# Slot transposes and slot weights from one bfloat16 product a quad, with the late one-hots formed in bfloat16 on VectorE

## The chip, the core and the metric

The kernel runs on one core of a Trainium2 chip. The metric is device time in microseconds; three runs of the kernel before took 504.05 us in the median (504.04 to 505.17). The engines are TensorE (PE; its weight loads are PEld), VectorE (DVE), ScalarE (ACT), GpSimd (POOL) and SyncE (SP, which only issues DMAs here).

## What is computed

A two-layer trunk for 256 tokens of width 1024. Each layer is a mixer and a mixture of experts (MoE), each followed by a layer norm of sqrt(2) times the input plus the result. The change lies in the MoE, which stands once in each layer:

```python
gate = jnp.sum(jax.nn.one_hot(expert_id, MOE_EXPERTS, dtype=f32) * weights[..., None], axis=1)
y = jnp.zeros((n_tok, d), f32)
for e in range(MOE_EXPERTS):
    hid = jax.nn.silu(t @ w_gate[e]) * (t @ w_up[e])
    y = y + gate[:, e:e + 1] * (hid @ w_down[e])
```

There are 16 experts in 4 groups. A router picks one group and two of its experts for each token, so all but two of a token's 16 gates are zero.

## The kernel before

The kernel doesn't compute every expert on every token. It cuts the tokens into two tiles of 128 (t = 0, 1) and gives every expert 32 slots in each tile, 512 slots in all. Four experts form a quad (q = 0 to 3), so a quad has 128 slots a tile.

For each tile, `rank` (L977) finds the slot numbers `pos` of a token's two experts, and `places` (L999) forms the one-hot matrix P of 128 tokens by 512 slots: `places(t, 0)` the columns of quads 0 and 1, `places(t, 1)`, later, those of quads 2 and 3. Products with P gather the tokens of the slots, transposed, into XT (`gather`, L1045). For each quad, `gate_up` (L1088) multiplies XT by the gate and up weights into the PSUM bank gu; `act` (L1100) forms sg = silu(gate) on ScalarE and hd = sg times up on VectorE; `turn` (L1108) transposes hd on TensorE (bank ht), and ScalarE copies it to hT; `down_mm` (L1119) multiplies by the down weights (bank dn); `weigh_hi` and `weigh_lo` multiply by the slot weight ws and split the result into a rounded part and a rest; `combine` adds PT times that to the tokens' sums. PT is P transposed by quads, and ws is the slot's gate, brought from token order into slot order.

`slots` (L1064) makes PT and ws. For each tile, TensorE transposes P in four pieces by the identity in fp32 (bank pt), and ScalarE copies the bank to PT; TensorE then multiplies each piece of P by rghl, the 16 gates of each token in two rounded parts (bank wsp), and VectorE adds the two parts and picks, for each of the four groups of 32 slots, the column of its own expert.

The order is written out by hand; each engine carries its instructions out in that order, and semaphores let one wait for another. Around the first quad it is: gates of both tiles, act of tile 0, the late halves of P, gate/up products of tile 1, its act, then on TensorE turn(0), slots(0), slots(1), turn(1) and the down products:

```python
        gates(0)
        gates(1)
        most()
        sc.preload_act_table_set(SILU)
        act(0, 0)
        places(0, 1)
        places(1, 1)
        acc = [None, None]
        gate_up(0, 1, range(8))
        act(0, 1)
        turn(0, 0)
        slots(0)
        slots(1)
        turn(0, 1)
        both(down, 0, 0)
```

PSUM banks for gu, ht, pt, wsp and dn come from one pool of four, so a bank's next writer waits for the last reader of what it held. Weights come in through a ring of 19 SBUF buffers that SP fills in order; two of the first quad's weight tiles (wh) are loaded by GpSimd's queue. After the gates, a token count (rcnti) is loaded into a register by every engine, for a branch on overfull experts that isn't taken with these inputs.

Of the kernel before, what the change touches and what calls it, by code (L numbers as in the profile page):

```python
# [9 lines left out]
F32 = mybir.dt.float32  # L10
F32R = mybir.dt.float32r
BF16 = mybir.dt.bfloat16
I32 = mybir.dt.int32
U32 = mybir.dt.uint32
AF = mybir.ActivationFunctionType
OP = mybir.AluOpType
# [25 lines left out]
for _n, _w in [("ident", 128), ("triU", 128), ("ntriSL", 128), ("sbT", 128),  # L42
               ("fold", 32), ("sel", 16), ("cosk", 32), ("sink", 32), ("ropeT", 256),
               ("e32p", 16), ("grp", 16), ("iota", 256), ("mssd", 128), ("msb", 128), ("mfox", 128), ("mmla", 128),
               ("ltri", 128), ("e32", 16)]:
    CC[_n] = (_o, _o + _w)
    _o += _w
NCC, NC0 = _o, CC["mssd"][0]
# [10 lines left out]
def constants():  # L59
    c = np.zeros((128, NCC), np.float32)  # L60

    def put(n, a):
        c[:a.shape[0], CC[n][0]:CC[n][1]] = a

    i = np.arange(128)
    r, k = i[:, None], i[None, :]
    f = np.float32
    put("ident", (r == k).astype(f))
    put("triU", (r <= k).astype(f))
    put("ntriSL", -(r > k).astype(f))  # L70
    put("sbT", -(r >= k).astype(f))
    put("fold", (r % 32 == np.arange(32)[None, :]).astype(f))
    h = np.arange(16)[None, :]
    put("sel", ((r % 32 == h) & (r < 96)).astype(f))
    inv = 10000.0 ** (-(np.arange(0, 32, 2, dtype=np.float64) / 32))
    inv = inv.astype(f)
    ang = (np.arange(256, dtype=f)[:, None] * inv[None, :]).astype(f).astype(np.float64)
    cos, sin = np.cos(ang).astype(f), np.sin(ang).astype(f)
    put("cosk", cos.reshape(2, 128, 16).transpose(1, 0, 2).reshape(128, 32))
    put("sink", sin.reshape(2, 128, 16).transpose(1, 0, 2).reshape(128, 32))  # L80

    put("ropeT", f(96.0 ** -0.5) * np.concatenate([np.ones((64, 256), f), cos.T, cos.T, -sin.T, sin.T]))
    put("mssd", np.where(r > k, f(NEG), f(0)))
    put("msb", np.where(r >= k, f(NEG), f(0)))
    put("mfox", np.where(k > r, f(NEG), f(0)))
    put("mmla", np.where(k // 64 > r // 64, f(NEG), f(0)))
    put("ltri", (r < k).astype(f))
    put("e32", np.broadcast_to(32.0 * np.arange(16, dtype=f), (128, 16)))
    put("e32p", np.broadcast_to(32.0 * np.arange(1, 17, dtype=f), (128, 16)))
    put("grp", np.broadcast_to(np.arange(16, dtype=f) // 4, (128, 16)))  # L90
    put("iota", np.broadcast_to(np.arange(256, dtype=f), (128, 256)))
    return c


class Builder:
# [21 lines left out]
    def S(self, shape, dt=F32, name="s", bufs=1):  # L117
        return self.sp.tile(shape, dt, tag=name, name=name, bufs=bufs)
# [145 lines left out]
    def make_constants(self):  # L264
        nc = self.nc
        v = nc.gpsimd
        self.ident = self.cv("ident")
        self.identb = self.cp.tile([128, 128], BF16, name="identb")
        v.tensor_copy(self.identb, self.ident)
        self.mask = {}  # L270
        for n in ("mssd", "msb", "mfox", "mmla"):
            self.mask[n] = self.cp.tile([128, 128], BF16, name=n)
            v.tensor_copy(self.mask[n], self.cv(n))
        one = self.cp.tile([128, 2], F32, name="one")
        v.memset(one[:, 0:1], 1.0)
        v.memset(one[:, 1:2], -1.0)
        self.one = one[:, 0:1]
        self.ones, self.nones = (one[:, k:k + 1].to_broadcast([128, 128]) for k in range(2))
        self.sbT = self.cp.tile([128, 128], F32R, name="sbT")
        v.tensor_copy(self.sbT, self.cv("sbT"))  # L280
        self.sel = self.cp.tile([128, 16], BF16, name="sel")
        v.tensor_copy(self.sel, self.cv("sel"))
        self.ltri = self.cp.tile([128, 128], BF16, name="ltri")
        v.tensor_copy(self.ltri, self.cv("ltri"))
        self.e32b = self.cp.tile([128, 16], BF16, name="e32b")
        v.tensor_copy(self.e32b, self.cv("e32"))
        self.onesb = self.cp.tile([128, 128], BF16, name="onesb")
        v.memset(self.onesb, 1.0)

# [638 lines left out]
    def moe(self, layer, seq0, mixer, tiles=0):  # L928
# [48 lines left out]
        def rank(t):  # L977
            r = R[t]
            rk = self.B("rk")
            pe.matmul(rk[:, :16], self.ltri, r["ab"], start=True, stop=False)  # L980
            pe.matmul(rk[:, :16], self.identb, self.e32b, start=False, stop=True)
            pe.matmul(rk[:, 16:32], self.onesb, r["ab"], start=True, stop=True)
            v.tensor_scalar(r["oh"][:, 1], iota16, r["ei"][:, 1:2], None, op0=OP.is_equal)
            ov = S([128, 16], name="rov", bufs=2)
            v.tensor_tensor(ov, rk[:, :16], self.cv("e32p"), op=OP.is_ge)
            pb = S([128, 16], name="rpb", bufs=2)
            v.scalar_tensor_tensor(pb, ov, 16384.0, rk[:, :16], op0=OP.mult, op1=OP.add)
            pos = S([128, 2], name="rpos", bufs=2)
            junk = S([128, 2, 16], name="rjk", bufs=2)
            for k in range(2):  # L990
                v.scalar_tensor_tensor(junk[:, k], r["oh"][:, k], 1.0, pb, op0=OP.mult, op1=OP.mult,
                                       accum_out=pos[:, k:k + 1])
            r.update(ov=ov, P=self.T([128, 512], F32R, name="P"), pos=pos)
            if "cnt" not in box:
                box["cnt"] = S([128, 2], name="rcnt")
            places(t, 0)
            v.tensor_reduce(box["cnt"][:, t:t + 1], rk[:, 16:32], axis=AX.X, op=OP.max)

        def places(t, h):  # L999

            r = R[t]
            P, pos, iota = r["P"][:, 256 * h:256 * h + 256], r["pos"], self.cv("iota")
            if h:
                v.tensor_scalar(pos, pos, -256.0, None, op0=OP.add)
            u = self.T([128, 256], name="P2")
            v.tensor_scalar(u, iota, pos[:, 1:2], None, op0=OP.is_equal)
            v.scalar_tensor_tensor(P, iota, pos[:, 0:1], u, op0=OP.is_equal, op1=OP.add)

        def most():

# [3 lines left out]
        def gates(t):  # L1014
# [12 lines left out]
            v.tensor_scalar(gate, r["oh"][:, 0], ng[:, 5:6], None, op0=OP.mult)  # L1027
            v.scalar_tensor_tensor(gate, r["oh"][:, 1], ng[:, 6:7], gate, op0=OP.mult, op1=OP.add)
            r["gate"] = gate
            r["ghl"] = g = S([128, 2, 16], F32R, name="rghl", bufs=2)  # L1030
            v.tensor_copy(g[:, 0], gate)
            v.tensor_sub(g[:, 1], gate, g[:, 0].bitcast(F32))

        def rows_hi(t):
            R[t]["rows"] = self.pair("rows")
# [25 lines left out]
            XT[t] = xt  # L1061

        def slots(t):
            p = R[t]["P"].bitcast(F32)  # L1064
            b = self.B("pt")
            for q in range(4):
                pe.transpose(b[:, 128 * q:128 * q + 128], p[:, 128 * q:128 * q + 128], self.ident)
            pt = self.T([128, 4, 128], F32R, name="PT")
            sc.activation(pt, b.rearrange("p (q n) -> p q n", q=4), AF.Copy)
            PT[t] = pt  # L1070
            b2 = self.B("wsp")
            for q in range(4):
                pe.matmul(b2[:, 36 * q:36 * q + 32], R[t]["P"][:, 128 * q:128 * q + 128], R[t]["ghl"].rearrange("p k n -> p (k n)"),
                          start=True, stop=True)
            ws = S([128, 4], name="ws", bufs=2)
            lo = S([128, 80], name="wlo")
            v.tensor_copy(lo[:, :64].rearrange("p (q n) -> p q n", n=16),
                          b2[:, :144].rearrange("p (q n) -> p q n", n=36)[:, :, 16:32])
            for e in range(4):
                r = slice(32 * e, 32 * e + 32)  # L1080

                v.tensor_tensor(ws[r], b2[r, :160].rearrange("p (q n) -> p q n", n=40)[:, :, e],
                                lo[r].rearrange("p (q n) -> p q n", n=20)[:, :, e], op=OP.add)
            WS[t] = ws

        gu, hid, yy = {}, {}, {}

# [20 lines left out]
        def turn(q, t):  # L1108
            b = self.B("ht")
            hd = hid.pop(t)  # L1110
            for k in range(2):
                pe.transpose(b[:, 128 * k:128 * k + 128], hd[:, 128 * k:128 * k + 128], self.ident)  # L1112
            ht = self.T([128, 2, 128], name="hT")
            sc.activation(ht, b[:, :256].rearrange("p (k n) -> p k n", k=2), AF.Copy)
            hid[t] = ht
# [112 lines left out]
        most()  # L1228
        sc.preload_act_table_set(SILU)
        act(0, 0)  # L1230
        places(0, 1)
        places(1, 1)
        acc = [None, None]
        gate_up(0, 1, range(8))
        act(0, 1)
        turn(0, 0)
        slots(0)
        slots(1)
        turn(0, 1)
        both(down, 0, 0)  # L1240
        self.reserve(2)
        n_max = nc.values_load(box["max"][0:1, 0:1], min_val=0, max_val=128)
# [615 lines left out]
```

## Time and profile before

| | |
|---|---|
| median of three runs | 504.05 us |
| the profiled execution | 505.15 us |
| its span, first to last instruction | 503.4 us |
| mean granted TensorE clock | 0.995 of full speed |
| first quad's gate/up to down, layer 0 | 189.44 to 191.74 us |
| the same in layer 1 | 406.36 to 408.66 us |
| matmuls of slots, both layers | 16 transposes (L1067), 16 weight products (L1073) |

The profile is of one execution. Times in it count from the start of its span. In a row of the timeline the columns are the start, the duration (of the whole row, where several instructions are merged as "x4"), the engine, the line of the kernel, the operation, output <- inputs by the program's names, and the shape; in brackets stands the idle time of the engine before it and what ended it. In a row of a group the columns behind the count are the busy time in us and the mean ns of one instruction.

### The profile page before, as it was taken

Reading aid. Unit: us, or ns where it says so; the run is one execution under the profiler, and the core shown is the slowest. Engines: PE = TensorE matmul, PEld = TensorE weight load, DVE = VectorE, ACT = ScalarE, POOL = GpSimd, SP = SyncE. Lnnn points to the kernel's source line nnn. Section 1 sums busy time; section 2 is a strip of 40 time slices with the busy share of each in tenths; the row PEclk is TensorE's granted clock in tenths of the full one; section 3 lists DMA queues with packets and bytes.
Section 4 is the critical chain, followed back from the end, with each engine's and each line's share of the span. In section 5 each row is a group of like instructions: output and inputs, shape, how many; then the busy total and the mean of one; then the engine's idle time right before and its main releaser. Section 6 shows DMA issues by size and latency. Waiting matters only on the chain. (4 is left out here: it accounts for less than half of the span.)

```text
span 503.4 us, 9615 instructions
## 1 busy us (share of the span) xinstructions
PE 486.5 (97%) x3805; PEld 315.5 (63%) x3805; DVE 301.6 (60%) x698; ACT 246.7 (49%) x512; POOL 74.6 (15%) x121
## 2 busy tenths in 40 slices
PE   8999999998999999999999999999999999999992
PEld 4999998886867634352333589988777442523330
DVE  4868957767966875152305786788677761411136
ACT  3788576667774434160303667556644351612031
POOL 0074000110000000070000097400000000520003
PEclk9999999999999999999999999999999999999998
DMA  8999952005348969999999792370578799999932
GB/s 313 419 421 416 422 204 85 0 1 201 135 133 332 417 241 425 419 423 420 421 418 415 300 421 103 154 251 1 169 250 317 292 423 422 422 420 421 416 133 83
DMA packets 21313, 146.97 MB, mean 292 GB/s; under 512 B 2385, under 2 KB 2641, under 8 KB 4113
## 3 DMA queue, kind: packets, MB, share of 16 engines
q1 hardware_dynamic: 20016, 140.16, 69.2%
q0 software_dynamic: 816, 5.51, 2.9%
q8 instruction: 31, 0.51, 0.4%
q10 hardware_dynamic: 432, 0.66, 0.4%
q14 instruction: 18, 0.14, 0.1%
HBM read 145.26 MB, written 1.05 MB: 291 GB/s over the span
## 5 line engine op out<-in xcount | busy, mean ns | idle before, releaser
L1095 PE MATMUL gu<-w,XT 128*32 128x512 f32 x960 | 106.5, 593 | 0.4 <-PEq L1320 0.4
L233 DVE TENSOR_TENSOR pair<-w,pair 128x1024 fp32r<-128x1024 f32 x58 | 71.1, 1230 | 17.2 <-ACT pair L232 16.6
L1095 PEld LDWEIGHTS gu<-w,XT 128*32 128x32 f32 x960 | 30.9, 110 | 67.0 <-issue 64.5
L232 ACT ACTIVATE pair<-w 128x1024 fp32r<-128x1024 f32 x58 | 61.3, 1059 | 7.4 <-PE qu L1542 2.8
L1125 PE MATMUL dn<-w,hT 128*32 128x512 f32 x512 | 57.4, 594 | 0.0
L1105 DVE TENSOR_TENSOR hd<-sg,gu 128x256 f32<-128x256 f32 x16 | 6.7, 420 | 69.1 <-ACT sg L1103 69.0
L1148 DVE SCALAR_TENSOR_TENSOR pair<-dn,ws,pair 128x512 fp32r<-128x512 f32 x28 | 21.0, 751 | 41.0 <-ACT pair L1142 39.1
L1103 ACT ACTIVATE sg<-gu 128x256 f32<-128x256 f32 x16 | 6.2, 385 | 78.4 <-PE gu L1095 78.3
L241 PE MATMUL ps<-xh,pair 128*128 128x256 f32 x288 | 41.5, 287 | 0.3 <-ACT pair L374 0.3
L244 PE MATMUL ps<-xl,pair 128*128 128x256 f32 x288 | 39.1, 278 | 0.0
L247 PE MATMUL ps<-xh,pair 128*128 128x256 f32 x288 | 39.0, 278 | 0.0
L241 PEld LDWEIGHTS ps<-xh,pair 128*128 128x128 f32 x288 | 36.1, 189 | 2.1 <-ACT pair L374 0.8
L1125 PEld LDWEIGHTS dn<-w,hT 128*32 128x32 f32 x512 | 15.4, 110 | 33.8 <-issue 29.8
L244 PEld LDWEIGHTS ps<-xl,pair 128*128 128x128 f32 x288 | 35.8, 188 | 0.0
L247 PEld LDWEIGHTS ps<-xh,pair 128*128 128x128 f32 x288 | 35.8, 188 | 0.0
L1142 ACT ACTIVATE pair<-dn,ws 128x512 fp32r<-128x512 f32 x28 | 19.3, 688 | 29.5 <-PE dn L1125 26.8
L1060 ACT ACTIVATE XT<-gp,pp 128x256 f32<-128x256 f32 x40 | 19.2, 564 | 17.8 <-PE gp L1053 17.7
L836 POOL TENSOR_TENSOR xres<-xres,w 128x256 f32<-128x256 f32 (+1 forms) x12 | 15.9, 1322 | 79.9 <-DVE rows L1041 79.9
L1605 ACT ACTIVATE pw<-z,sm 128x128 f32<-128x128 f32 (+1 forms) x32 | 13.1, 420 | 17.8 <-DVE sm L1602 17.8
L316 PE MATMUL vp<-pair,xh 128*128 128x256 f32 x128 | 20.0, 289 | 1.8 <-DVE pair L233 1.6
L316 PEld LDWEIGHTS vp<-pair,xh 128*128 128x128 f32 x128 | 16.7, 188 | 3.1 <-DVE pair L233 2.0
L431 DVE SCALAR_TENSOR_TENSOR cy<-ps,pp,cy 128x255 f32<-128x255 f32 (+2 forms) x36 | 17.3, 480 | 2.0 <-ACT cy L428 1.1
(378 smaller groups left out, 902.3 us busy)
## 6 DMA issues: line engine op xcount, KB each, us to landing
w<-in_wgu_dram SPq DMA_DIRECT2D x60, 1024.0 KB, 11.6
w<-in_wd_dram SPq DMA_DIRECT2D x32, 1024.0 KB, 13.3
w<-in_w_dram SPq DMA_DIRECT2D x15, 1024.0 KB, 18.4
w<-in_wout_dram SPq DMA_DIRECT2D x10, 1024.0 KB, 17.5
wh<-in_wgu_dram POOLq DMA_DIRECT2D x4, 1024.0 KB, 7.3
w<-in_ln_dram SPq DMA_DIRECT2D x4, 1024.0 KB, 13.8
w<-in_wfox_dram SPq DMA_DIRECT2D x4, 1024.0 KB, 8.8
w<-in_wfv_dram SPq DMA_DIRECT2D x2, 1024.0 KB, 18.9
```

The source lines that it names most:

```text
L232: self.nc.scalar.activation(vh, src, AF.Copy)
L233: (self.nc.gpsimd if pool else self.nc.vector).tensor_tensor(vl, src, vh.bitcast(F32), op=OP.subtract)
L241: mm(ps, hi[:, c, :], xh[:, c, :], start=(c == 0), stop=False)
L244: mm(ps, hi[:, c, :], xl[:, c, :], start=False, stop=False)
L247: mm(ps, lo[:, c, :], xh[:, c, :], start=False, stop=(c == n - 1))
L316: mm(o, xx[:, 4 * k + c, 128 * t:128 * t + 128], ww[:, c, :], start=(k == 0 and n == 0), stop=(k == 1 and n == 11))
L431: v.scalar_tensor_tensor(y[:, k:], ps[:, :256 - k], self.pp[:, i:i + 1], y[:, k:], op0=OP.mult, op1=OP.add)
L1060: sc.activation(xt[:, c, :], b[:, i], AF.Identity, bias=bb, scale=g)
L1095: pe.matmul(gu[t][32 * e:32 * e + 32, :], XT[t][:, c, o:o + 32], w[:, e, :], start=(c == 0), stop=(c == 7))
L1125: pe.matmul(b[32 * e:32 * e + 32, :], ht[:, k, 32 * e:32 * e + 32], w[:, e, :], start=(k == 0), stop=(k == 1))
L1142: sc.activation(y, dn[t, s], AF.Copy, scale=WS[t][:, q:q + 1])
L1148: v.scalar_tensor_tensor(yl, b, WS[t][:, q:q + 1], yh.bitcast(F32), op0=OP.mult, op1=OP.subtract)
```

## The change

The matrix product of `slots` is taken once for each quad and tile, in bfloat16: the stationary side is a bfloat16 copy P16 of the quad's 128 columns of P, and the moving side, ridg, is the identity (128 columns) next to the gates in three bfloat16 parts (3 x 16 columns). Its first 128 columns are the transposed P, the other 48 the gates of each slot in three parts. Two quads share a bank. The slot weight is picked by one multiplication by a 0/1 mask (qm, which marks each slot's expert) and a sum over the 48 columns. `gates` forms three parts in place of two, with the identity copied in by GpSimd. The late half of the one-hots is formed in bfloat16 (two comparisons and a sum) directly into P16; ScalarE copies the early half into P16, and GpSimd copies the late half back into the fp32 P, which the later gathers read. turn(0, 1) now stands between slots(0) and slots(1). Two constants are new: qm, loaded with the other constants, and a bfloat16 copy of the column numbers.

```diff
+        self.qm = self.cp.tile([128, 64], BF16, name="qm")
+        v.tensor_copy(self.qm, self.cv("qm"))
+        self.iota16 = self.cp.tile([128, 256], BF16, name="iota16")
+        v.tensor_copy(self.iota16, self.cv("iota"))
...
+        def places_16(t):
+            r = R[t]
+            r["P16"] = p = self.T([128, 512], BF16, name="P16")
+            sc.activation(p[:, :256], r["P"][:, :256].bitcast(F32), AF.Copy)
+            pos, u = r["pos"], self.T([128, 256], BF16, name="P2")
+            v.tensor_scalar(pos, pos, -256.0, None, op0=OP.add)
+            v.tensor_scalar(u, self.iota16, pos[:, 1:2], None, op0=OP.is_equal)
+            v.tensor_scalar(p[:, 256:], self.iota16, pos[:, 0:1], None, op0=OP.is_equal)
+            v.tensor_tensor(p[:, 256:], p[:, 256:], u, op=OP.add)
+            nc.gpsimd.tensor_copy(r["P"][:, 256:], p[:, 256:])
...
-            r["ghl"] = g = S([128, 2, 16], F32R, name="rghl", bufs=2)
-            v.tensor_copy(g[:, 0], gate)
-            v.tensor_sub(g[:, 1], gate, g[:, 0].bitcast(F32))
+            r["idg"] = g = S([128, 176], BF16, name="ridg", bufs=2)
+            nc.gpsimd.tensor_copy(g[:, :128], self.identb)
+            rest = S([128, 16], name="rpb", bufs=2)
+            v.tensor_copy(g[:, 128:144], gate)
+            v.tensor_sub(rest, gate, g[:, 128:144])
+            v.tensor_copy(g[:, 144:160], rest)
+            v.tensor_sub(g[:, 160:], rest, g[:, 144:160])
...
         def slots(t):
-            p = R[t]["P"].bitcast(F32)
-            b = self.B("pt")
-            for q in range(4):
-                pe.transpose(b[:, 128 * q:128 * q + 128], p[:, 128 * q:128 * q + 128], self.ident)
...
+            p = R[t].pop("P16")
             pt = self.T([128, 4, 128], F32R, name="PT")
...
+            for h in range(2):
+                bank = self.B("pt")
+                b = bank[:, :352].rearrange("p (q n) -> p q n", q=2)
+                for k in range(2):
+                    q = 2 * h + k
+                    pe.matmul(b[:, k], p[:, 128 * q:128 * q + 128], R[t]["idg"], start=True, stop=True)
+                sc.activation(pt[:, 2 * h:2 * h + 2], b[:, :, :128], AF.Copy)
+                for k in range(2):
+                    q = 2 * h + k
+                    m = self.qm[:, None, 16 * q:16 * q + 16].to_broadcast([128, 3, 16])
+                    w = b[:, k, 128:].rearrange("p (i n) -> p i n", i=3)
+                    v.scalar_tensor_tensor(junk, w, 1.0, m, op0=OP.mult, op1=OP.mult, accum_out=ws[:, q:q + 1])
...
-        places(0, 1)
-        places(1, 1)
+        places_16(0)
+        places_16(1)
...
+        turn(0, 1)
         slots(1)
-        turn(0, 1)
```

The order of instructions on three engines, in layer 0 (layer 1 has the same). First TensorE, from the last gate/up products of tile 1 to the first down products. Before:

```order
L1095 MATMUL gu<-wh,XT 32x512 x8
L1112 MATMUL ht<-cc,hd 128x128 x2
L1067 MATMUL pt<-cc,P 128x128 x4
L1073 MATMUL wsp<-rghl,P 128x32 x4
L1112 MATMUL ht<-cc,hd 128x128 x2
L1125 MATMUL dn<-w,hT 32x512 x16
```

Here the rows pt and wsp stand twice before the second ht, for tiles 0 and 1. In the changed kernel, with the semaphores that each waits for in brackets (P_2256 is P16 of tile 1):

```order
L1132 MATMUL ht<-cc,hd 128x128 [waits DVE_49,Activation_49]
L1132 MATMUL ht<-cc,hd 128x128
L1096 LDWEIGHTS P_2256
L1096 MATMUL pt<-ridg,P_2256 128x176 [waits Pool_49]
L1096 LDWEIGHTS P_2256 [waits DVE_49]
L1096 MATMUL pt<-ridg,P_2256 128x176 [waits Activation_49]
L1145 MATMUL dn<-w,hT 32x512 [waits DMAHW2_49,Activation_49]
```

The second ht now stands ahead of tile 1's products (each LDWEIGHTS and MATMUL pair stands twice). Behind the names are these instructions: ht waits for VectorE's second hd and for ScalarE's copy of the first ht; the third product of tile 1 for VectorE's second mask product, which is the last reader of the bank; the first dn for ScalarE's copy of the second ht, the last reader of its bank.

Next VectorE, from tile 1's gates to the second hd (buffer numbers kept). Before:

```order
L1031 CAST rghl_2226<-rgate_2223 128x16
L1032 TENSOR_TENSOR rghl_2226<-rgate_2223,rghl_2226 128x16
L1012 TENSOR_TENSOR rcnti_2229<-rcnt_2000 128x1
L1105 TENSOR_TENSOR hd_2234<-sg_2232,gu_2069 128x256
L1004 TENSOR_SCALAR rpos_1995<-rpos_1995 128x2
L1006 TENSOR_SCALAR P2_2237<-cc_97,rpos_1995 128x256
L1007 SCALAR_TENSOR_TENSOR P_1999<-cc_97,rpos_1995,P2_2237 128x256
L1004 TENSOR_SCALAR rpos_2152<-rpos_2152 128x2
L1006 TENSOR_SCALAR P2_2241<-cc_97,rpos_2152 128x256
L1007 SCALAR_TENSOR_TENSOR P_2156<-cc_97,rpos_2152,P2_2241 128x256
L1105 TENSOR_TENSOR hd_2291<-sg_2289,gu_2244 128x256
```

In the changed kernel:

```order
L1052 TENSOR_TENSOR rpb_2236<-rgate_2231,ridg_2234 128x16
L1053 CAST ridg_2234<-rpb_2236 128x16
L1054 TENSOR_TENSOR ridg_2234<-rpb_2236,ridg_2234 128x16
L1029 TENSOR_TENSOR rcnti_2241<-rcnt_2004 128x1
L1125 TENSOR_TENSOR hd_2246<-sg_2244,gu_2073 128x256
L1020 TENSOR_SCALAR rpos_1999<-rpos_1999 128x2
L1021 TENSOR_SCALAR P2_2250<-iota16_371,rpos_1999 128x256
L1022 TENSOR_SCALAR P16_2248<-iota16_371,rpos_1999 128x256
L1023 TENSOR_TENSOR P16_2248<-P16_2248,P2_2250 128x256
L1020 TENSOR_SCALAR rpos_2156<-rpos_2156 128x2
L1021 TENSOR_SCALAR P2_2258<-iota16_371,rpos_2156 128x256
L1022 TENSOR_SCALAR P16_2256<-iota16_371,rpos_2156 128x256
```

Each tile's gates have two rows more, and each late one-hot has four rows where it had three. Behind the second hd, eight mask products (L1103) stand where two copies and eight short sums stood.

Last GpSimd, between its loads of the first quad's weights and the count. Before, nothing lies between the two loads and TENSOR_LOAD; in the changed kernel:

```order
L165 DMA wh<-in_wgu_dram 128x2048 x2
L1049 COPY ridg<-identb 128x128 x2
L1024 CAST P<-P_2248 128x256
L1024 CAST P<-P_2256 128x256
L1262 TENSOR_LOAD rcnti
```

The two copies of the identity wait for nothing but their place in the queue; the two casts wait for VectorE's late one-hots.

More of the change, by code (lines that the diff above doesn't have):

```diff
@@ L44 @@
                ("e32p", 16), ("grp", 16), ("iota", 256), ("mssd", 128), ("msb", 128), ("mfox", 128), ("mmla", 128),
-               ("ltri", 128), ("e32", 16)]:
+               ("ltri", 128), ("e32", 16), ("qm", 64)]:
     CC[_n] = (_o, _o + _w)
@@ L90, in constants @@
     put("grp", np.broadcast_to(np.arange(16, dtype=f) // 4, (128, 16)))
+    put("qm", (np.arange(16)[None, None, :] == 4 * np.arange(4)[None, :, None] + i[:, None, None] // 32)
+        .astype(f).reshape(128, 64))
     put("iota", np.broadcast_to(np.arange(256, dtype=f), (128, 256)))
@@ L995, in rank, with places @@
                 box["cnt"] = S([128, 2], name="rcnt")
-            places(t, 0)
+            places(t)
             v.tensor_reduce(box["cnt"][:, t:t + 1], rk[:, 16:32], axis=AX.X, op=OP.max)
[L999 to L1004, printed above, removed]
+        def places(t):
+            P, pos, iota = R[t]["P"][:, :256], R[t]["pos"], self.cv("iota")
             u = self.T([128, 256], name="P2")
@@ L1063, in slots @@
         def slots(t):
-            p = R[t]["P"].bitcast(F32)
-            b = self.B("pt")
-            for q in range(4):
-                pe.transpose(b[:, 128 * q:128 * q + 128], p[:, 128 * q:128 * q + 128], self.ident)
+            p = R[t].pop("P16")
             pt = self.T([128, 4, 128], F32R, name="PT")
[L1069 to L1074, printed above, removed]
-            ws = S([128, 4], name="ws", bufs=2)
[L1076 to L1084, printed above, removed]
+            ws = S([128, 4], name="ws", bufs=2)
+            junk = S([128, 3, 16], BF16, name="wsj")
+            for h in range(2):
[10 more added lines that the diff above has]
+                    v.scalar_tensor_tensor(junk, w, 1.0, m, op0=OP.mult, op1=OP.mult, accum_out=ws[:, q:q + 1])
+            PT[t], WS[t] = pt, ws
         gu, hid, yy = {}, {}, {}
```

## The prediction

> **What bounds the kernel now.** I read the page first, then the waits of TensorE, then the timeline around the work that the change rewrites.
>
> ```profile
> span 503.4 us, 9615 instructions
> PE 486.5 (97%) x3805; PEld 315.5 (63%) x3805; DVE 301.6 (60%) x698; ACT 246.7 (49%) x512; POOL 74.6 (15%) x121
> ```
>
> TensorE is busy for 97% of the span. In the list of what TensorE waited for, the longest entry of the whole run is
>
> ```profile
> PE vp L316 <- DVE pair L233: 1.6, 2, 1.3
> ```
>
> and none names a DMA. So time that TensorE loses or gains anywhere goes to the end almost one for one. The work in question stands once in each layer, between the first quad's gate/up products and its first down product. In layer 0:
>
> ```profile
> 187.61 1.90 PE L1095 MATMUL gu<-wh,XT 128*32 128x512 f32 x16
> 189.44 0.44 PE L1112 MATMUL ht<-cc,hd 128*128 128x128 f32 x2
> 189.72 0.60 PE L1067 MATMUL pt<-cc,P 128*128 128x128 f32 x4
> 190.07 0.60 PE L1073 MATMUL wsp<-rghl,P 128*128 128x32 f32 x4
> 190.52 0.66 PE L1067 MATMUL pt<-cc,P 128*128 128x128 f32 x4
> ...
> 191.38 0.44 PE L1112 MATMUL ht<-cc,hd 128*128 128x128 f32 x2
> 191.74 1.06 PE L1125 MATMUL dn<-w,hT 128*32 128x512 f32 x8
> ```
>
> The columns are start, duration, engine, line, operation. Eight transposes (pt) and eight weight products (wsp) take TensorE from 189.72 to 191.38, 1.66 us, without a gap. Layer 1 repeats it to the hundredth: 2.30 us from the first ht to the first dn, as 191.74 - 189.44 here.
>
> ```profile
> 406.36 0.44 PE L1112 MATMUL ht<-cc,hd 128*128 128x128 f32 x2
> 408.66 7.07 PE L1125 MATMUL dn<-w,hT 128*32 128x512 f32 x64
> ```
>
> So I work out by how much the first dn of layer 0 moves, and count it twice.
>
> **What is removed on TensorE.** Sixteen fp32 products become eight bfloat16 ones of 176 columns.
>
> ```profile
> 71.89 0.27 PE L293 MATMUL e<-mssd,identb 128*128 128x256 bf16 x1
> 72.00 0.33 PE L474 MATMUL e<-lrow,sel 128*128 128x384 bf16 x1
> ```
>
> A bfloat16 product of 256 columns holds TensorE 0.11 us (72.00 - 71.89), so 176 columns hold it about 0.08: 8 x 0.08 = 0.64 us where 1.66 stood. TensorE's own work falls by 1.0 us a layer. This is not the gain, because the second ht now stands after four of these products, not after sixteen others, and it needs hd of the second token tile from VectorE, and that needs sg from ScalarE.
>
> **When VectorE reaches the second hd.** Call that moment T; it is 190.17 now.
>
> ```profile
> 187.16 0.17 DVE L1031 CAST rghl<-rgate 128x16 fp32r<-128x16 f32 x1
> 187.37 0.17 DVE L1032 TENSOR_TENSOR rghl<-rgate,rghl 128x16 fp32r<-128x16 f32 x1
> 187.46 0.15 DVE L1012 TENSOR_TENSOR rcnti<-rcnt 128x1 int32<-128x1 f32 x1
> 187.85 0.42 DVE L1105 TENSOR_TENSOR hd<-sg,gu 128x256 f32<-128x256 f32 x1 [0.24 <-ACT sg L1103]
> 188.19 0.16 DVE L1004 TENSOR_SCALAR rpos<-rpos 128x2 f32<-128x2 f32 x1
> 188.39 0.35 DVE L1006 TENSOR_SCALAR P<-cc,rpos 128x256 f32<-128x256 f32 x1
> 188.78 0.48 DVE L1007 SCALAR_TENSOR_TENSOR P<-cc,rpos,P 128x256 fp32r<-128x256 f32 x1
> 189.18 0.16 DVE L1004 TENSOR_SCALAR rpos<-rpos 128x2 f32<-128x2 f32 x1
> 190.17 0.41 DVE L1105 TENSOR_TENSOR hd<-sg,gu 128x256 f32<-128x256 f32 x1
> ```
>
> Three pieces. (1) The gate weights are split in three, not two: two more dependent small instructions a tile. A dependent one follows after 0.21 us (187.16 to 187.37), an independent one after 0.09 (187.37 to 187.46). Four more are 0.84, so rcnti moves from 187.46 to 188.30 and the first hd can start at 188.39. Its sg moves too, since tile 0's two extra ones delay ScalarE's part of tile 1's gates, the table load and sg by 0.42:
>
> ```profile
> 187.44 0.38 ACT L1103 ACTIVATE sg<-gu 128x256 f32<-128x256 f32 x1
> 189.58 0.39 ACT L1103 ACTIVATE sg<-gu 128x256 f32<-128x256 f32 x1 [1.76 <-PE gu L1095]
> 189.92 0.38 ACT L1114 ACTIVATE hT<-ht 128x256 f32<-128x256 f32 x1
> ```
>
> sg then ends at 187.44 + 0.42 + 0.38 = 188.24, before 188.39. So the first hd is late by 188.39 - 187.85 = 0.54. (2) The late one-hots take 0.99 us a tile now (188.19 to 189.18). Four instructions replace three. No row shows these forms; the nearest are
>
> ```profile
> L303 DVE CAST lrow<-rest 16x256 bf16<-16x256 f32 x2 | 0.6, 284 | 0.1
> L1516 DVE COPY lrow<-lrow 128x128 bf16<-128x128 bf16 x1 | 0.2, 195 | 0.0
> ```
>
> A comparison of 256 columns should lie between the copy of half the length, 0.195, and the fp32 comparison, 0.35; I take 0.29, the cast of 256 columns. The sum of two one-hots lies between L1032 (0.17 for 16 columns) and hd (0.42 for 256 in fp32); I take 0.29 as well. Rpos to the next is 0.20 (188.19 to 188.39); an instruction that doesn't wait starts 0.08 before its forerunner's end (hd: 0.42 long, next after 0.34), one that waits 0.04 after it. That makes 0.20 + 0.21 + 0.33 + 0.21 = 0.95 a tile: 0.08 gained over both, bounds +0.5 (all as long as fp32: 0.20 + 0.27 + 0.39 + 0.34 = 1.20 a tile) and -0.6 (0.20 + 0.12 + 0.24 + 0.09 = 0.65). T = 190.17 + 0.54 - 0.08 = 190.63. (3) GpSimd now copies each late one-hot back to fp32, the first copy about when VectorE starts on tile 1's.
>
> ```profile
> 320.17 0.84 DVE L1614 TENSOR_SCALAR pw<-pw,sm 128x128 f32<-128x128 f32 x1
> 320.19 0.73 POOL L837 TENSOR_TENSOR xres<-xres,w 128x256 f32<-128x256 f32 x1
> 321.19 0.27 DVE L1614 TENSOR_SCALAR pw<-pw,sm 128x128 f32<-128x128 f32 x1
> L269 POOL CAST identb<-cc 128x128 bf16<-128x128 f32 x1 | 0.3, 292 | 0.0
> L282 POOL CAST sel<-cc 128x16 bf16<-128x16 f32 x1 | 0.2, 201 | 0.0
> ```
>
> The same scalar operation takes 0.27 us alone and 0.84 beside a GpSimd operation. The copy itself is 0.40 by the two casts (0.81 ns a column). By the steps above tile 0's one-hot ends at 189.76 and tile 1's first comparison is due at 189.88; sg ends at 187.82 and hd starts at 187.85, so a hand-over costs at least 0.03, and the two start almost together. I charge 0.2, half a copy; bounds 0 and 0.57, the loss in the L1614 row. T = 190.83.
>
> The Trainium skill speaks against this part: SBUF — State Buffer, section "SBUF: two separate sides", says that VectorE in its two-port modes and GpSimd take one port pair as an exclusive lock, and the loser waits out the whole instruction. By that rule the whole 0.40 is lost when GpSimd is first and nothing when VectorE is. The 0.84 row agrees that waiting is near total.
>
> **From T to the first dn.** By the program's waits, the first dn needs the PSUM buffer of the second ht, so it waits for ScalarE's second hT copy; and the third product of tile 1 needs the buffer of tile 0's first pair, so it waits for VectorE's first two mask products (each takes its accumulator out too), which wait for ScalarE's first PT half, which waits for tile 1's one-hot.
>
> ```profile
> 482.69 0.38 PE L1112 MATMUL ht<-cc,hd 128*128 128x128 f32 x2
> 483.11 0.38 ACT L1114 ACTIVATE hT<-ht 128x256 f32<-128x256 f32 x1 [1.62 <-PE ht L1112]
> L961 DVE SCALAR_TENSOR_TENSOR rL<-lg,mv,rbias 128x24 f32<-128x24 f32 x4 | 1.0, 239 | 0.1
> L991 DVE DVE_READ_ACCUMULATOR rjk<-roh,rpb 128x1 f32 x8 | 0.6, 81 | 0.0
> ```
>
> First chain: hd 0.41, to TensorE 0.06 (twice the smallest hand-over), ht until its copy starts 0.42, hT 0.38, back 0.06: T + 1.33. Second: the one-hot ends at T + 0.08, a PT half takes 0.42 with its wait, each mask product 0.36 (0.24 + 0.08 + 0.04), then back 0.06 and two products 0.18: T + 0.08 + 0.42 + 0.72 + 0.06 + 0.18 = T + 1.46. Both are near; with the second, dn starts at 190.83 + 1.46 = 192.29 against 191.74: 0.55 us later, although TensorE has 1.0 us less to do. Nothing further down is late: ScalarE reads the first slot weight behind the first eight dn products, at least 1.06 us after dn starts, and it is there at T + 0.9; the third dn bank, 16 products or 1.77 us after dn starts (a quarter of the 7.07 above), needs the sixth mask product, which ends at T + 0.5 + 6 x 0.36 = T + 2.7, against T + 3.2.
>
> **The other edits.** ScalarE's two P16 copies (0.4 each, as hT) stand between 188.2 and 189.0, in the gap of 1.76 us ahead of its second sg; without the gap each would cost its 0.4. The constants grow by 32 KB and two GpSimd casts, at a time when TensorE waits for no load: 0 to 0.1. GpSimd's two copies of the identity now run right behind its wh load, beside the router's chain:
>
> ```profile
> 162.98 0.53 POOL L162 DMA_DIRECT2D wh<-in_wgu_dram  x1 [2.07 <-PE lg L958]
> 167.12 0.48 DVE L1007 SCALAR_TENSOR_TENSOR P<-cc,rpos,P 128x256 fp32r<-128x256 f32 x1
> 167.72 0.19 PEld L1052 LDWEIGHTS gp<-P,rows 128*128 128x128 f32 x1
> ```
>
> P ends at 167.60 and the gather starts at 167.72, so a loss of 0.29 there (one copy) would cost some 0.2; bounds 0 and 0.5 (both copies); I take 0.1, and only in layer 0, since layer 1's wh load stands earlier against its gather. GpSimd's count load and its router load queue behind the casts; they have no reader soon. On SP the count load waits 0.84 longer, and what is queued behind it, the gain rows, waits for a ring buffer that only the dn products free.
>
> **Sum.** 2 x 0.55 + 0.1 = +1.2 us. The profiled execution took 505.15 us, 1.75 of them around its span of 503.4; it would become 506.35. The three timed runs were 504.04, 504.05 and 505.17, so I add the 1.2 to their median: 505.2. About 0.3%, 1.5 us, is what a measurement of this kernel can tell from no change.
>
> **Rivals.** *TensorE's saving arrives in full*: 2 x 1.0 less, 502.0. Against it stands the chain sg, hd, ht, hT: sg of tile 1 can't end before 189.97, so T is 190.0 at best. Chance 0.04, for waits that I misread. *VectorE is quicker than costed*, near the lower bounds, so that T falls to 190.0 to 190.1: dn at 191.5, 0.25 earlier a layer, 503.5. Chance 0.15. *The port decides (slower)*: tile 1's first comparison loses as much as L1614 did, 0.57 in place of 0.2, and the router's chain 0.4: 2 x 0.92 + 0.4 = +2.2, 506.3. It decides from the point where GpSimd's first copy starts ahead of 189.88. Chance 0.22. *bfloat16 gains nothing on VectorE*: T is later by another 0.5 + 0.08, so 2 x (0.55 + 0.58) + 0.1 = +2.4, 506.4. Chance 0.11.
>
> **How the numbers follow.** The forecast holds 0.48. Low end: the quick rival, 503.5; high end: the two slow rivals, 506.5. Faster by over 0.3%: 0.04. Slower: most of the two slow rivals, 0.29, and a share of the forecast's own spread, 0.05, 0.34. Within: 0.62.
>
> **What would show it.** Right: TensorE idle about 1 us ahead of the second ht, ended by hd, and again ahead of tile 1's third product or of dn; the first hd 0.5 later behind tile 1's gates; comparisons at 0.29. Wrong: no idle there and dn near 190.7 (first rival), or comparisons near 0.2 (second) or 0.8 (third). If TensorE waits for a load or a PSUM bank elsewhere, the step "one for one" is wrong.

## The result, and the profile after

| | median | ratio to before, 95% interval |
|---|---|---|
| before | 504.15 us | |
| changed | 511.88 us (511.03 to 512.14) | 1.0144 [1.0131, 1.0157] |

The changed kernel is 7.7 us slower where 1.2 was forecast, and outside the range. The profiled execution of before was a long one (505.15 us against a median of 504.15), that of the changed kernel was not (511.77), so the two spans differ by 6.6 us only. The page of its profile, with the two lines that answer to those of before:

```profile
span 510.0 us, 9645 instructions
PE 488.5 (96%) x3789; PEld 316.3 (62%) x3789; DVE 303.1 (59%) x722; ACT 247.5 (49%) x520; POOL 76.0 (15%) x131
```

TensorE is busy for 2.0 us more although it has 16 products less. I set the starts of the same products of both executions side by side, to see where the 6.6 us of span come in:

| product | before | changed | behind by | added here |
|---|---|---|---|---|
| xh times pair, first mixer | 34.48 | 34.51 | 0.03 | |
| yo, end of the first mixer | 79.95 | 80.97 | 1.02 | 1.0, step by step, with no wait |
| first dn, layer 0 | 191.74 | 193.19 | 1.45 | 0.43 |
| vp, second mixer | 301.66 | 303.07 | 1.41 | |
| the vp behind it | 301.78 | 305.18 | 3.40 | 1.99, a wait |
| ku, second mixer | 310.29 | 315.85 | 5.56 | 2.16, slow products |
| first dn, layer 1 | 408.66 | 414.93 | 6.27 | 0.71, of which 0.50 in the changed stage |
| end | 503.4 | 510.0 | 6.6 | |

Only the third and seventh rows are places that the prediction speaks of. There the timeline (start, duration, engine, line, operation) reads, in layer 0 (the last two rows are the ends of the same stage in layer 1):

```profile
188.60 1.90 PE L1115 MATMUL gu<-wh,XT 128*32 128x512 f32 x16
189.35 0.41 DVE L1125 TENSOR_TENSOR hd<-sg,gu 128x256 f32<-128x256 f32 x1
189.69 0.16 DVE L1020 TENSOR_SCALAR rpos<-rpos 128x2 f32<-128x2 f32 x1
189.88 0.29 DVE L1021 TENSOR_SCALAR P<-iota,rpos 128x256 bf16<-128x256 bf16 x1
190.43 0.44 PE L1132 MATMUL ht<-cc,hd 128*128 128x128 f32 x2
190.61 0.16 DVE L1020 TENSOR_SCALAR rpos<-rpos 128x2 f32<-128x2 f32 x1
190.71 0.47 PE L1096 MATMUL pt<-ridg,P 128*128 128x176 bf16 x4
190.81 0.50 DVE L1021 TENSOR_SCALAR P<-iota,rpos 128x256 bf16<-128x256 bf16 x1
190.83 0.40 POOL L1024 CAST P<-P 128x256 fp32r<-128x256 bf16 x1 [25.85 <-DVE rpos L1020]
191.75 0.41 DVE L1125 TENSOR_TENSOR hd<-sg,gu 128x256 f32<-128x256 f32 x1
192.31 0.41 PE L1132 MATMUL ht<-cc,hd 128*128 128x128 f32 x2 [1.14 <-DVE hd L1125]
193.19 3.21 PE L1145 MATMUL dn<-w,hT 128*32 128x512 f32 x28
...
412.13 0.44 PE L1132 MATMUL ht<-cc,hd 128*128 128x128 f32 x2
414.93 2.35 PE L1145 MATMUL dn<-w,hT 128*32 128x512 f32 x20
```

This is what was forecast: TensorE idle for 1.14 us ahead of the second ht, ended by hd, and 2.76 us from the first ht to the first dn (193.19 - 190.43) where 2.30 stood, 2.80 in layer 1 (414.93 - 412.13). The larger loss lies elsewhere. In the list of TensorE's waits two entries are new in their size, ht and the wait of vp for ScalarE's pair (0.2 us in all before):

```profile
PE ht L1132 <- DVE hd L1125: 2.3, 2, 1.2
PE vp L323 <- ACT pair L235: 2.1, 2, 1.8
```

and the timeline of ScalarE and TensorE at that place, 110 us behind the changed code, shows where it comes from:

```profile
299.42 0.86 ACT L1546 ACTIVATE cu<-ct,pp 128x128 f32<-128x128 f32 x3
303.66 0.52 ACT L1548 ACTIVATE cthl<-cu 128x384 fp32r<-128x384 f32 x1 [3.38 <-issue]
304.08 1.04 ACT L235 ACTIVATE pair<-w 128x1024 fp32r<-128x1024 f32 x1
305.18 0.74 PE L323 MATMUL vp<-pair,xh 128*128 128x256 f32 x4 [1.83 <-ACT pair L235]
```

ScalarE stood still for 3.38 us between two small instructions, and "issue" says that no semaphore, tile or DMA which the profile shows held it. The weight strip (pair) behind it came late, and TensorE waited for that. What followed is seen in two windows (from:to, length, busy time and number of products, granted clock):

```profile
303.00:307.00 4.00, 2.10 (x16) 0.99 0.67 281
307.00:310.30 3.30, 3.30 (x18) 0.50 0.00 0
```

TensorE was idle for about half of 4 us, and in the next 3.3 us its clock was halved: 18 products fit there, against 32 in a stretch of the same length about that place in run e2 below (305.0 to 308.3 us), at a clock of 1.00. The Trainium skill (TensorE: Matmul & The Clock Gate, Part 1: The HAM clock gate) has half rate after an idle window of some 3.4 us. Here the longest idle time was 1.83 us, which is shorter, so the trace doesn't bear that length out.

How long TensorE waits doesn't decide this alone. A wait of 1.3 us stands near 116 us in the profiles of all fourteen kernels of this document. In twelve the clock stays at 1.00 behind it; in those of e4 and e11 below it was halved there too, 0.51 in the mean from 117.5 to 121.0 us of e4. First before, then e4:

```profile
116.14 1.21 PE L316 MATMUL vp<-pair,xh 128*128 128x256 f32 x8 [1.32 <-DVE pair L233]
```

```profile
117.13 1.73 PE L322 MATMUL vp<-pair,xh 128*128 128x256 f32 x8 [1.29 <-DVE pair L235]
```

The eight products behind the wait take 1.21 us in the one and 1.73 in the other. What decides between the two isn't shown.

Last, the loss of 1.0 us with no wait. Before, and then changed, in groups of eight products of the first mixer:

```profile
52.39 1.07 PE L244 MATMUL ps<-xl,pair 128*128 128x256 f32 x8
53.30 1.07 PE L247 MATMUL ps<-xh,pair 128*128 128x256 f32 x8
```

```profile
52.70 1.10 PE L247 MATMUL ps<-xl,pair 128*128 128x256 f32 x8
53.65 1.10 PE L250 MATMUL ps<-xh,pair 128*128 128x256 f32 x8
```

Eight products take 0.91 us (52.39 to 53.30) before and 0.95 (52.70 to 53.65) after: steps of about 114 and 118 ns, at full clock in both.

### The profile page after: what moved, and what is told of

The parts are those of the page before. It is cut to its first block, busy times and chain, and to the rows that moved or that the text cites. A ratio compares the mean times of both kernels' runs of the same rounds, so it can differ in the third digit from the quotient of the medians.

```text
span 510.0 us, 9645 instructions
## 1 busy us (share of the span) xinstructions
PE 488.5 (96%) x3789; PEld 316.3 (62%) x3789; DVE 303.1 (59%) x722; ACT 247.5 (49%) x520; POOL 76.0 (15%) x131
## 5 line engine op out<-in xcount | busy, mean ns | idle before, releaser
L323 PE MATMUL vp<-pair,xh 128*128 128x256 f32 x128 | 21.1, 299 | 3.8 <-ACT pair L235 2.1
```

The lines of the kernel that those rows point to most:

```text
L323: mm(o, xx[:, 4 * k + c, 128 * t:128 * t + 128], ww[:, c, :], start=(k == 0 and n == 0), stop=(k == 1 and n == 11))
```

## The experiments

| run | kernel | median | ratio to before, 95% interval |
|---|---|---|---|
| e1 | before, ScalarE's branch 9 instructions later | 508.13 | 1.0066 [1.0049, 1.0082] |
| e9 | before, 3 instructions later | 505.88 | 1.0032 [1.0018, 1.0047] |
| e2 | changed, 96 ScalarE instructions in the branch not taken | 507.71 | 1.0063 [1.0046, 1.0080] |
| e3 | e2, one-hot of tile 1 behind the second hd | 506.25 | 1.0040 [1.0025, 1.0055] |
| e4 | before, with the two constants | 506.69 | 1.0042 [1.0028, 1.0056] |
| e5 | before, 640 bytes of empty room | 506.74 | 1.0050 [1.0034, 1.0065] |
| e11 | before, 128 bytes | 506.90 | 1.0048 [1.0031, 1.0064] |
| e12 | before, 256 bytes | 504.58 | 1.0000 [0.9990, 1.0009] |
| e10 | before, 512 bytes | 504.28 | 0.9999 [0.9990, 1.0009] |
| e6 | before, the two constants behind the buffers | 504.56 | 1.0004 [0.9995, 1.0013] |
| e7 | e2, the two constants behind the buffers | 506.05 | 1.0030 [1.0018, 1.0042] |
| e8 | e3, the two constants behind the buffers | 504.25 | 0.9993 [0.9984, 1.0002] |

**ScalarE's stall.** In layer 0 each engine comes to the branch for overfull experts and jumps over its body. ScalarE's branch stands six instructions later in the changed kernel: two copies of P16, one more copy of PT a tile, and two waits. The DMA view lists two queues of the kind "instruction", which bring code in blocks. It doesn't say for which engine a block is; that q14, with blocks of 8 KB, serves ScalarE is inferred from what follows. For the windows 245 to 258 us, about the branch (249.8 us before, 251.3 changed), and 298 to 308 us, the row of q14 (count, MB, share) reads before

```profile
q14 instruction: 2, 0.02, 0.3%
...
q14 instruction: 1, 0.01, 0.3%
```

and in the changed kernel

```profile
q14 instruction: 1, 0.01, 0.2%
...
q14 instruction: 2, 0.02, 0.5%
```

One block fewer is fetched about the branch and one more where ScalarE stands still. The theory from this: branch and target now lie in one block, nothing is fetched at the jump, and ScalarE runs into the end of what it holds. Two runs test it from both sides. The first leaves the computation of the kernel before as it is and only adds ScalarE instructions ahead of the branch:

```diff
                 sc.activation(y, dn[t, s], AF.Copy, scale=WS[t][:, q:q + 1])
+                for _ in range(2 * (layer == 0 and (q == 0 or (q, t) == (1, 0)))):
+                    sc.activation(y[:, :16], dn[t, s][:, :16], AF.Copy, scale=WS[t][:, q:q + 1])
```

> The kernel before, with twelve extra ScalarE instructions of 16 columns (two behind each scaled copy of the first quad and of tile 0 of the second, layer 0 only). With the semaphore instructions that fall away, ScalarE's branch of layer 0 stands nine instructions later in its code; in the changed kernel it stands six later. Theory A (code position): in the changed kernel ScalarE ran out of loaded code 57 instructions behind that branch, because the branch and its target fell into one block of code, so that no new block was fetched at the jump. Then this kernel shows the same: ScalarE idle about 3.4 us for nothing that the profile shows, some 3 instructions before the place of the changed kernel, at 296 to 302 us; TensorE's wait at vp about 2 us; granted clock 0.992 in place of 0.995; 504.15 + 4.0 = about 508. Theory B (the stall belongs to the changed code or its data: P16, the new tiles, GpSimd): no such stall, 504 to 505; the extra instructions of 0.2 us lie where ScalarE is idle half of the time.

Measured: 508.13 us, with the stall on ScalarE, a wait of 2.7 us on TensorE and the halved clock (0.992 mean):

```profile
297.57 0.35 ACT L1528 ACTIVATE cu<-ct,pp 128x128 f32<-128x128 f32 x1
302.12 0.63 ACT L1528 ACTIVATE cu<-ct,pp 128x128 f32<-128x128 f32 x2 [4.20 <-issue]
```

The stall falls on another line than in the changed kernel, but on the same count: the 383rd ScalarE instruction of the record in both, semaphore instructions counted. The second run adds instructions to the changed kernel's branch body, where they are never executed:

```diff
-                sc.activation(sg, gu[:, :256], AF.Silu)
+                for _ in range(4):
+                    sc.activation(sg, gu[:, :256], AF.Silu)
```

> The changed kernel, with 96 more ScalarE instructions in each layer inside the overflow branch, which isn't taken: nothing more is executed, but ScalarE's code behind the branch stands 96 instructions later. Theory A (code position): the jump now goes to another block, the next block is fetched ahead, ScalarE's 3.4 us stall at about 300 us is gone, TensorE doesn't wait 1.8 us there, and the clock isn't halved for 3.4 us; the time falls by 4.0, from 511.9 to about 507.9, granted clock 0.995. Theory B (the stall belongs to the changed code or its data): 511.9, with the stall where it was.

Measured: 507.71 us, as theory A had it. The stall is gone, and at the same place ScalarE goes on at once:

```profile
301.76 0.86 ACT L1547 ACTIVATE cu<-ct,pp 128x128 f32<-128x128 f32 x3
302.66 0.53 ACT L1549 ACTIVATE cthl<-cu 128x384 fp32r<-128x384 f32 x1
```

Its q14 rows for the two windows:

```profile
q14 instruction: 3, 0.02, 0.5%
...
q14 instruction: 1, 0.01, 0.2%
```

One of its three blocks comes ahead of the branch (245 to 251 us), so two come behind it, as before; e1 has the counts of the changed kernel, 1 and 2. Theory B, that the stall belongs to the changed code or its data, falls by both runs. A third run asks how near the kernel before stood to this (the edit of the first run, without "2 *" and the loop):

> The kernel before with six extra ScalarE instructions of 16 columns in layer 0 (one behind each scaled copy of the first quad and of tile 0 of the second); three semaphore instructions fall away, so the branch stands three instructions later. In the changed kernel and in the run with nine ScalarE stalled at the same recorded instruction, the 383rd, although those are different instructions of the program. Theory A (blocks of code): if the kernel before just escaped, with its branch among the last of a block, three are enough: a stall of 3.4 to 4.2 us at the 383rd instruction, which is now the second of the three copies cu of tile 1, at 300 to 301 us, and 507.5 to 508.5. If blocks are not what counts, but the amount of added work: 504.3 to 504.8, no stall.

```profile
299.44 0.35 ACT L1528 ACTIVATE cu<-ct,pp 128x128 f32<-128x128 f32 x1
301.82 0.63 ACT L1528 ACTIVATE cu<-ct,pp 128x128 f32<-128x128 f32 x2 [2.03 <-issue]
```

The place was right: the 383rd instruction, the second copy of tile 1. The size was not: 2.03 us, no halved clock, and 505.88 where 507.5 to 508.5 was expected. TensorE's wait for ScalarE's pair stays at 0.2 us there; the loss shows a little later, at qu, where a wait of 0.5 us on VectorE's pair is new. So three instructions suffice, and what a stall costs depends on how long it is and on the slack where it falls.

Two more things stand in the traces. In all three stalls ScalarE goes on 1.8 to 1.9 us behind the start of a q14 block (301.89 us for 303.66 in the changed kernel, 300.25 for 302.12 in e1, 300.06 for 301.82 in e9). That block starts 1.6, 2.3 and 0.3 us after ScalarE has stopped, which is how the lengths of the stalls differ; what sets its start isn't shown. And right behind the branch of layer 0 each engine carries out a BRANCH_PREFETCH_HINT, the kernel's own, in every run. ScalarE reaches it 0.19 us behind the branch in the three kernels that stall and 0.46 to 0.48 us behind it in all others. That fits a jump that fetches nothing, but no run leaves the hint out, so its part in the stall is open.

The Trainium skill (Runtime: NRT & Kernel Launch, Instruction fetch mechanics) says that a jump to a target outside the blocks held stalls the engine for a fetch. These runs show a different case: a jump that seems to stay within a block costs nothing at the jump, and 2 to 4 us at the end of that block. That no block is fetched ahead after such a jump is inferred from the counts of q14. What e1, e2 and e9 show is that the place of ScalarE's code decides whether it stalls.

**The slower products.** The constants alone, in the kernel before:

> The kernel before with the change's constants alone: 32 KB more in the constant load, the two new tiles and their two casts on GpSimd; nothing reads them. In the changed kernel TensorE's products of the first mixer step by 118 ns from 32 to 80 us where 114 ns stood in the kernel before, 0.95 us in all, with no wait between. Theory C (place of the tiles in the on-chip memory, moved by the new constants): the same here, 118 ns and about +0.9 us, 505.0. Theory D (it differs from one execution to the next, or comes from the code): 504.1, and the step is 114 ns, or differs with no relation to the constants.

Measured 506.69, +2.3 us, with steps of 118 ns; theory C, but dearer than I thought. Room alone, with nothing loaded or added, tells placement from load:

```diff
-        self.onesb = self.cp.tile([128, 128], BF16, name="onesb")
+        self.onesb = self.cp.tile([128, 128 + 320], BF16, name="onesb")[:, :128]
```

> The kernel before with 640 bytes of unused room behind its constants in each partition, the room that the change's two new constant tiles take: every buffer for split weights, tokens and small tiles moves by 640 bytes, and no instruction or load is added. The run of the constants alone took +2.3 us (506.69 against 504.41), of which 1.1 us are products at steps of 118 ns where 114 ns stood, from 38 to 80 us. Theory C (place of the tiles): the same here, 118 ns from 38 to 80 us and +1.1 to +2.3 us, 505.5 to 506.7. Theory D (the load or the casts of the constants, or the execution): 504.4 and 114 ns.

```profile
52.87 1.10 PE L244 MATMUL ps<-xl,pair 128*128 128x256 f32 x8
53.81 1.10 PE L247 MATMUL ps<-xh,pair 128*128 128x256 f32 x8
```

506.74 us and the slow step (0.94 us for eight): the place is what costs. Set beside run e10 below, which is as quick as before, e5 starts the same product 0.21 us later at 9 us (8.96 against 8.75) and 1.99 later at 79 us (81.13 against 79.14), with no new wait between; from 330 to 370 us it loses another 0.4. So slow steps make up most of the 2.4 us. The counterpart keeps load and casts and puts the two tiles behind the buffers:

```diff
-        self.qm = self.cp.tile([128, 64], BF16, name="qm")
+        self.qm = self.S([128, 64], BF16, name="qm")
...
-        self.iota16 = self.cp.tile([128, 256], BF16, name="iota16")
+        self.iota16 = self.S([128, 256], BF16, name="iota16")
```

> The kernel before with the change's constants loaded and cast, but the two new tiles stand behind the buffers (in the pool of the small tiles, the last one), so that the buffers for weights and tokens stay where they were. Theory C (place): 504.4, steps of 114 ns from 38 to 72 us. Theory D (load or casts): 506.7, as the run of the constants alone.

504.56 us, 1.0004 [0.9995, 1.0013]: load and casts cost nothing that can be measured. Three more sizes of empty room show which displacement matters:

> The kernel before with 512 bytes of unused room behind the constants, where 640 cost 2.4 us. If the place within 512 bytes decides (640 = 512 + 128), this is as the kernel before, 504.3, with steps of 114 ns from 38 to 72 us. If any other place is worse, 506 to 507 and 118 ns.

> The same with 128 bytes. If the place within 512 bytes decides, this is as 640 bytes, 506.7, with steps of 118 ns; if the distance decides, nearer to 504.3.

> The kernel before with 256 bytes of unused room behind the constants. 128 and 640 bytes cost 2.4 us, 512 none, so the place within 512 bytes decides; which half is the good one isn't known. If 256 is as 512: 504.4; as 128: 506.8. If it is better than both, products at 114 ns also where the kernel before has 118, the time would fall below 504, at best by some 2 us.

With 512 bytes eight products take 0.91 us again, and with 256 too; with 128 they take 0.94:

```profile
52.48 1.07 PE L247 MATMUL ps<-xh,pair 128*128 128x256 f32 x8
53.39 1.07 PE L241 MATMUL ps<-xh,pair 128*128 128x256 f32 x8
```

```profile
53.18 1.10 PE L244 MATMUL ps<-xl,pair 128*128 128x256 f32 x8
54.12 1.10 PE L247 MATMUL ps<-xh,pair 128*128 128x256 f32 x8
```

(first e10, then e11). 0, 256 and 512 bytes cost nothing, 128 and 640 cost 2.4 us: the place within 256 bytes decides, not the distance. Only multiples of 128 were tried. I had guessed 512, and hoped that one of them might be better than the kernel before; none is. Which buffer's place it is, and why the read slows, stays open: not every product is slow in the one and quick in the other, and a stretch of some us has one step throughout. The profiled execution of before has the slow step too in its first stretch, 0.94 us for eight (10.82 to 11.76).

**The change itself.** With the code moved and the constants behind the buffers, what is left is what the prediction summed:

> The changed kernel with the 96 instructions in the branch that isn't taken, and with the two constants behind the buffers: what is left is the change of slots itself and its waits. Theory C: 507.7 less 1.1 to 2.3, 505.4 to 506.6; the forecast's own sum on the kernel before (504.4 + 1.2 = 505.6) would then hold for what it summed. Theory D: 507.7.

506.05 us, 1.0030 [1.0018, 1.0042]: 1.5 us [0.9, 2.1] over the kernel before, where 1.2 was forecast. Its first quad, layer 0 and layer 1:

```profile
188.97 0.44 PE L1132 MATMUL ht<-cc,hd 128*128 128x128 f32 x2
190.85 0.41 PE L1132 MATMUL ht<-cc,hd 128*128 128x128 f32 x2 [1.14 <-DVE hd L1125]
191.73 1.06 PE L1145 MATMUL dn<-w,hT 128*32 128x512 f32 x8
...
406.37 0.44 PE L1132 MATMUL ht<-cc,hd 128*128 128x128 f32 x2
408.30 0.41 PE L1132 MATMUL ht<-cc,hd 128*128 128x128 f32 x2 [1.16 <-DVE hd L1125]
409.18 1.07 PE L1145 MATMUL dn<-w,hT 128*32 128x512 f32 x8
```

2.76 and 2.81 us from the first ht to the first dn, 0.46 and 0.51 over the 2.30 of before. The chain through VectorE that the prediction names can be cut by order alone:

```diff
         places_16(0)
-        places_16(1)
         acc = [None, None]
         gate_up(0, 1, range(8))
         act(0, 1)
+        places_16(1)
         turn(0, 0)
         slots(0)
         turn(0, 1)
-        slots(1)
         both(down, 0, 0)
+        slots(1)
```

> As the run before, and tile 1's late one-hot stands behind the second hd on VectorE, its products behind the first down products of tile 0 on TensorE. If the chain from VectorE to the second ht is what costs the 0.55 us a layer, the second hd starts when its sg is there (about 0.75 us earlier), the second ht follows, and the first dn starts right behind it: 1.2 to 1.4 us a layer earlier, 2.4 to 2.8 in all against the run before. If the 0.55 us came from elsewhere (PSUM banks, ScalarE's copies), at most 0.5 us are gained.

> As the run before, and tile 1's late one-hot behind the second hd, its products behind tile 0's down products. The same step took 1.5 us off (507.71 to 506.25): 505.6 less 1.5 = 504.1 by theory C, at best 503.5, so about 0.1 to 0.2% faster than the kernel before, near what can be measured; by theory D 506.2.

They took 1.5 and 1.8 us off; from e3 2.4 to 2.8 had been expected, from e8 the 1.5 of e3. In e8:

```profile
189.96 0.44 PE L1132 MATMUL ht<-cc,hd 128*128 128x128 f32 x2 [0.29 <-DVE hd L1125]
190.32 3.64 PE L1145 MATMUL dn<-w,hT 128*32 128x512 f32 x32
193.90 0.48 PE L1096 MATMUL pt<-ridg,P 128*128 128x176 bf16 x4
194.30 1.06 PE L1145 MATMUL dn<-w,hT 128*32 128x512 f32 x8
```

The idle time ahead of ht is 0.29 in place of 1.14 and the first dn is 1.41 earlier (191.73 to 190.32), but tile 1's four products now stand behind the first 32 dn products, and 0.40 us of that goes back (193.90 to 194.30). I had counted the first dn as the gain. e8, at 504.25 us, is not told apart from the kernel before (504.28 in the same runs), so no version here beats it.

## Why the prediction was wrong

**The sum of the changed stage was right, in part by luck.** The first hd starts 0.75 us behind tile 1's last gate/up rows (189.35 - 188.60) where 0.24 stood: 0.51 later, 0.54 forecast. A late one-hot takes 0.92 (189.69 to 190.61), 0.95 forecast, with comparisons at 0.29. GpSimd's copy meets the first comparison of tile 1 as feared, which takes 0.50 in place of 0.29: 0.21 lost, 0.2 charged; in layer 1 it takes 0.43. The second hd is 3.15 behind the gate/up rows (191.75 - 188.60) against 2.56: 0.59 later, 0.66 forecast. From there to dn it takes 1.44 (193.19 - 191.75), 1.46 forecast. A layer loses 0.46 and 0.50, 0.55 forecast.

Two of these terms came out for another reason than the one given. The 1.46 was the chain through the mask products; the first dn ended up waiting for the other chain, ScalarE's second hT, which had been costed at 1.33 and took 1.44:

```profile
192.88 0.11 PEld L1096 LDWEIGHTS <-P 128*128 128x128 bf16 x2 [0.23 <-DVE wsj L1103]
193.19 0.16 PEld L1145 LDWEIGHTS dn<-w,hT 128*32 128x32 f32 x8 [0.20 <-ACT hT L1134]
```

The mask products follow each other after 0.25 us (192.36 to 192.61) where 0.36 was charged, so tile 1's third product starts 1.13 behind hd, 1.28 forecast. And the 0.2 for GpSimd was charged as half a copy, against the rule that the prediction quotes from the Trainium skill (SBUF — State Buffer, "SBUF: two separate sides"). The trace agrees with that rule: the comparison ends 0.08 us behind the copy in both layers (191.31 behind 191.23; 413.05 behind 412.97), as it did in the row of L1614 (320.17 + 0.84 = 321.01 behind 320.92). So VectorE waits out the copy, and what it loses is set by where the copy ends; whether the comparison runs in one of the two-port modes that the rule names isn't shown. That is not the whole 0.40, as the prediction read the rule: of two that start together, one of 0.40 and one of 0.29, it makes 0.40 + 0.08 - 0.29 = 0.19.

The rivals of this stage had their answer too: no full saving on TensorE, comparisons neither near 0.2 nor near 0.8.

**The step that failed is "The other edits".** It costed ScalarE's two P16 copies at nothing, by the idle time that hides them, and the constants at 0 to 0.1 us, by the 32 KB and two casts. Both are right for the work, and e6 shows it for the constants. But an instruction is also code, and a tile is also room. The six ScalarE instructions moved a branch, to a place where ScalarE later stalls: 4.1 us (1.0144 less 1.0063), a stall of 3.38, of which TensorE waited 1.83, and then a halved clock for some 3.3 us. The two tiles moved every buffer behind them by 640 bytes: 1.7 us here (1.0063 less 1.0030), 2.4 in the kernel before. With the 1.5 us of the stage these make 7.3 us, the 1.44% of the ratio, as differences of ratios must; that each has its cause is shown by the runs that took it out (e2, then e7). Why the block is missed, and why the place of a buffer slows a read, stays open.

**The range failed with it.** All four rivals were cases of the changed stage (one with the router's chain), and so was each bound. The text named a wait elsewhere as what would make it wrong, but gave it no price. The step "one for one" held: TensorE's lost time went to the end, and more than that, since the wait of 1.83 us was followed by another 2.2 lost at half clock.

The 0.1 us for the router's chain did not show: in the table above nothing is added between 80 us and the first quad.

## What to carry to other kernels

When a change adds instructions to an engine that later jumps, or bytes ahead of the big buffers, its effect isn't confined to its stage: compare the starts of the same products over the whole span first, and read "issue" gaps and steps of equal products before explaining the stage that was edited. Before judging such a change, take these two out: fill a branch that isn't taken, and put new constants behind the buffers or round their room up to 256 bytes. And a wait of 2 us on TensorE can cost twice that when a halved clock follows. Behind a wait of 1.3 us the halved clock came in two of fourteen profiles, so look for it before comparing two of them.

## What the runs showed of the hardware

ScalarE can stand still for 2.0 to 4.2 us in straight code, 55 to 61 recorded instructions behind a branch, by the place of its code (e1, e9, and the changed kernel, all at the 383rd recorded instruction). The same products of 128 x 256 step at about 114 or 118 ns by where the buffers lie within 256 bytes, 2.4 us in 504 for 128 bytes. A halved granted clock for some 3.4 us followed a wait of 1.83 us in the changed kernel, of 2.7 in e1 and of 1.3 in e4 and e11, and did not follow the same wait of 1.3 us in the kernel before. And a VectorE comparison that met a GpSimd copy ended 0.08 us behind it in both layers.
